# A hybrid decoder layer on one core: both value heads in one product, a shorter inverse root, smaller tiles and a new order

## The chip, the cores and the metric

The kernel runs on one core of a Trainium2 chip. The metric is device time in microseconds (us) of one launch; less is better. Engines are named as in the profile: PE is TensorE's matrix products, PEld its weight loads, DVE is VectorE, ACT is ScalarE, POOL is GpSimd, SP is the queue that issues all DMAs here. PSUM is the memory that products land in, in banks of 128 x 512 float32.

## What is computed

The reference, cut to what the change touches:

```python
h = _rmsnorm(x, norm_w)                    # x: (1, 4096, 1024)
u = (h @ w_in)                             # one projection for both groups
# GLA group: 4 heads, key 64, value 128, chunked, gated
o = _gla_chunked(q, k, v, log_a)
o = o * rsqrt(mean(o*o) + eps) * gla_norm_w
gla_out = o * silu(gg)
# RWKV group: 8 heads of 64, delta rule, step by step over t
kk = kk / max(norm(kk), 1e-12)
S = S*w_t + (S @ -kk_t) (kk_t*a_t)^T + v_t k_t^T ;  y_t = S r_t
y = (y - mean) * rsqrt(var + eps) * ln_w + ln_b
rwkv_out = (y + bonus) * silu(rg)
out = _rmsnorm(x + concat(gla_out, rwkv_out) @ w_out, final_norm_w)
```

The kernel computes the RWKV recurrence in chunks of 64 steps. In a chunk the step-by-step rule becomes products with the inverse of a 64 x 64 triangular matrix, which is called N below.

## The kernel before

**Tiles and stages.** The 4096 positions are cut into 8 blocks of 512 (`TB`). For each block `x_block` normalises x and splits it into a high and a low float16 part; every projection is three float16 products (high by high, high by low, low by high), each of 8 row tiles, for 128 output columns of the weight. A pair of heads is a unit: `rwkv_ab` prepares the 32 RWKV units (8 blocks, 4 pairs), `rwkv_i` finishes the inverse N, `rwkv_c` runs the recurrence over the 8 chunks of a unit, and `rwkv_d` norms its output. `gla_proj` makes keys, queries, values and gates of the 16 GLA units (8 blocks, 2 pairs), and `gla_pair` does their chunks. `out_block` is the output projection, `out_last` that of the last block. The weights are read once, scaled and split by `split_w` and `split_o` in the first part of the program, written to DRAM (`wdr`) and loaded again for each block.

**How products use the array.** `duo` and `both` issue two products that use one half of the array's output columns each (the profile writes 128\*64) and run side by side. The values are made the other way round than all else: x is the stationary operand, and the value weight of one head is the moving one, 128 columns at a time (`gla_proj`, the loop over m, t and the three parts). The transposes use the full array (128\*128), the sums over partitions a quarter (128\*32), the products of 64 rows half of it the other way (64\*128), and the inverse 32\*32.

**The recurrence.** For each chunk `rwkv_c` does three products that hang on each other: `ch<-sv,DD` (state by keys), `ch<-us,Nb` (by N) and `ch<-uv,bk` (new state). Between them ACT copies `us` and `uv` out of PSUM, and DVE makes the next `sv`. N lies in `Nb`, of 192 columns for a chunk: the two heads' blocks stand on the diagonal of a 128 x 128 square with zeros beside them, and the last 64 columns hold a second matrix.

**The inverse.** POOL runs the triangular solve of 32 x 32 blocks (`Tc`, `tm`); its input goes through DRAM (`nd`) and its output through DRAM (`td`, four DMAs) back into `Nb`. `rwkv_i` transposes blocks on DVE (`Ta`) and does two sets of small products.

**The norms.** `newton` makes an inverse square root on DVE from an integer first guess and two Newton steps, eight instructions in all, of 128 x 128. Its result lies in a few rows; `bcast` spreads these over all partitions by DRAM, and `spread` by products with the columns of the tile `sel`, which four small DMAs fill at the start.

**What sets the order.** The code runs as nine streams; a recorder notes each instruction, and a planner gives them the order in which they are issued. Each engine then takes its own in that order and waits on semaphores. The starting times come from a table (`STARTS`), and the planner improves on them with costs of its own. `NW` and `NXR` are numbers of buffers: three of value, key, query and gate weights (`wg`), two of x (`xr`). All recorded instructions stand on line 626 in the profile, or on line 685 when `duo` issues them, so the rows are read by tile.

The values before, with the lines of the profile:

```python
1374            for m in range(2):
1375                i = W_V + 2 * j + m
1376                w = yield from get_w(i)
...
1379                for t in range(4):
1380                    for m_, (a, c) in enumerate(((0, 0), (0, 1), (1, 0))):
...
1383                        for k in range(KT):
...
1385                            both(ps[:, t, :], xs[k][:, c, P * t:P * t + P], w[a][:, k, :], ...
```

Of the kernel before, what the change touches and what calls it, by code (L numbers as in the profile page):

```python
# [1823 lines left out]
```

## Time and profile before

| | |
|---|---|
| median of 3 runs | 2205.69 us (2202.84 to 2206.76) |
| profiled execution, span | 2206.1 us |
| PE busy | 2119.0 us, 96% |
| PEld busy | 1352.7 us, 61% |
| DVE busy | 1711.7 us, 78% |
| ACT busy | 1253.8 us, 57% |
| POOL busy | 875.1 us, 40% |
| DMA | 326.90 MB, 148 GB/s |

The profiled execution has no time of its own beside its span; the span lies 0.4 us above the median of the timed runs and inside their spread, so span and time are read as one here. The share of busy time is an average over parts with different limits, and a matmul's recorded length includes the time in which it drains while the next one already runs.

### The profile page before, as it was taken

What the parts mean: (1) busy time and instruction counts of PE and PEld (TensorE: products, weight loads), DVE (VectorE), ACT (ScalarE), POOL (GpSimd) and SP (SyncE); (2) the same over time, 40 slices, a digit from 0 to 9 for tenths busy, and PEclk for the clock granted to TensorE, in tenths of its full rate; (3) what the DMA queues carried; (4) which work ended last, traced back from release to release, by engine and by line L of the source; (5) the groups of instructions that cost most, each with busy time, mean ns of one, the idle gap of its engine ahead of it and who ended that gap; (6) DMA issues with size and microseconds to landing.
All of it is one profiled execution on the core that took longest, in us unless ns stands there. A gap on an engine that the chain in (4) does not pass through costs nothing.

```text
span 2206.1 us, 75003 instructions
## 1 busy us (share of the span) xinstructions
PE 2119.0 (96%) x30680; PEld 1352.7 (61%) x30680; DVE 1711.7 (78%) x3802; ACT 1253.8 (57%) x3229; POOL 875.1 (40%) x2212
## 2 busy tenths in 40 slices
PE   7888999999999999999999999999999999999997
PEld 3555665566755657556575666656666566756664
DVE  7888969688784977867877886867878578785876
ACT  7766675564645546554654546545465465555452
POOL 3454233625244352335525354441543525254400
PEclk9999999999999999999999999999999999999999
DMA  6786556455344643456444654355544465345443
GB/s 201 230 249 205 182 160 178 141 177 167 91 123 142 184 141 98 115 145 188 138 114 116 183 154 129 101 131 165 164 117 124 127 190 160 90 117 140 130 123 97
DMA packets 275454, 326.90 MB, mean 148 GB/s; under 512 B 131572, under 2 KB 132772, under 8 KB 275108
## 3 DMA queue, kind: packets, MB, share of 16 engines
q1 hardware_dynamic: 275108, 322.10, 50.8%
q8 instruction: 240, 3.93, 0.8%
q14 instruction: 106, 0.87, 0.1%
HBM read 276.94 MB, written 45.05 MB: 146 GB/s over the span
## 4 chain that ended last, share of the span: by engine, by line
PE 66%; DVE 16%; DMA 9%; issue 2%; ACT 2%; SPq 2%; POOL 2%; DVEq 0%; POOLq 0%; ACTq 0%
PE bank L685 52%; PE bank L626 8%; PE ch L685 4%; DMA xr<-in_xT_dram 2%; SPq L626 2%; DVE DD L626 2%; DVE nta L626 1%; DVE bk L626 1%; PE y L626 1%; DMA rn<-bcda 1%; DMA x<-in_wt_dram 1%; PE y L685 1%; DVE mgg L626 1%; DVE x L626 1%; DVE Nb L626 1%
## 5 line engine op out<-in xcount | busy, mean ns | idle before, releaser
L685 PE MATMUL bank<-x,wr 128*64 128x512 f16 x6528 | 796.2, 380 | 7.2 <-ACT x L626 1.4
L626 POOL TENSOR_TENSOR tm<-Tc,f 128x60 f32<-128x60 f32 (+24 forms) x961 | 347.7, 362 | 589.0 <-DMA f<-nd 507.2
L685 PEld LDWEIGHTS <-wr 128*64 128x64 f16 x6528 | 356.1, 110 | 260.1 <-issue 22.1
L626 POOL TENSOR_TENSOR Tc<-Tc,tm 128x60 f32<-128x60 f32 (+24 forms) x961 | 358.2, 373 | 74.1
L685 PE MATMUL bank<-x,wg 128*64 128x512 f16 x3072 | 367.1, 381 | 3.0 <-DMA wg<-wdr 1.9
L685 PE MATMUL bank<-x,wo 128*64 128x512 f16 x2976 | 357.2, 380 | 0.0
L626 POOL TENSOR_TENSOR xacc<-xacc,xr 128x512 f32<-128x512 f32 x98 | 130.8, 1334 | 359.5 <-ACT xr L626 227.9
L685 PEld LDWEIGHTS <-wg 128*64 128x64 f16 x3072 | 169.4, 110 | 126.3 <-issue 5.0
L626 DVE SCALAR_TENSOR_TENSOR sv<-ch,PC,psd 64x64 f32<-64x64 f32 x434 | 122.5, 282 | 160.1 <-PE ch L685 140.6
L685 PEld LDWEIGHTS <-wo 128*64 128x64 f16 x2976 | 159.2, 110 | 112.4 <-issue 2.9
L685 PEld LDWEIGHTS <-x 128*64 128x64 f16 x6240 | 190.1, 111 | 20.8 <-issue 9.0
L685 PE MATMUL bank<-wg,x 128*64 128x128 f16 x6144 | 195.4, 220 | 4.6 <-DMA wg<-wdr 3.0
L626 ACT ACTIVATE psd<-sv,PC 128x128 f32<-128x128 f32 x248 | 98.9, 399 | 139.4 <-DVE sv L626 108.3
L626 ACT COPY uv<-ch 64x64 f32<-64x64 f32 x496 | 102.3, 206 | 76.5 <-PE ch L685 69.5
L626 ACT COPY us<-ch 64x64 f32<-64x64 f32 x496 | 102.2, 206 | 67.8 <-PE ch L685 57.7
L626 ACT ACTIVATE sa<-bank,mu_s 128x512 f32<-128x512 f32 x104 | 71.6, 689 | 73.5 <-PE bank L685 71.1
L626 DVE COPY_PREDICATED Nb<-mc,bank 64x512 f32<-64x512 uint8 x128 | 92.8, 728 | 13.1 <-PE bank L626 11.3
L626 POOL MEMSET Tc<- 32x8 f32 (+1 forms) x160 | 24.2, 151 | 186.1 <-DMA td<-Tc 180.7
L626 DVE COPY_PREDICATED DD<-mc,bank 64x512 f32<-64x512 uint8 x128 | 93.3, 731 | 2.3
L685 PEld LDWEIGHTS ch<-uv,bk 128*64 128x64 f32 x992 | 66.1, 137 | 44.1 <-ACT uv L626 10.9
L685 PEld LDWEIGHTS ch<-us,Nb 128*64 128x64 f32 x992 | 65.4, 137 | 43.0 <-ACT us L626 11.0
L685 PEld LDWEIGHTS ch<-sv,DD 128*64 128x64 f32 x992 | 65.0, 136 | 40.0 <-DVE sv L626 7.3
(348 smaller groups left out, 3611.8 us busy)
## 6 DMA issues: line engine op xcount, KB each, us to landing
wr<-wdr SPq DMA_DIRECT2D x256, 256.0 KB
wg<-wdr SPq DMA_DIRECT2D x184, 256.0 KB
xr<-in_xT_dram SPq DMA_DIRECT2D x176, 256.0 KB
wo<-wdr SPq DMA_DIRECT2D x128, 256.0 KB
f<-nd SPq DMA_DIRECT2D x128, 128.0 KB
x<-in_wt_dram SPq DMA_DIRECT2D x29, 512.0 KB
wdr<-wo SPq DMA_DIRECT2D x25, 512.0 KB
out_dram<-mgg SPq DMA_DIRECT2D x33, 256.0 KB
```

The costliest lines, as they stand in the source:

```text
L626: put(t0, self.name, d, lag, cols, tiles, tab, outs, ins, lambda: f(*a, **kw))
L685: nc.tensor.matmul(x, lhsT=l, rhs=y, start=start, stop=stop)
```

## The change

It makes these edits:

- **Values.** The weights of both heads of a pair are loaded into neighbouring buffers, and one product streams both, 256 columns at a time, for two of the four row tiles in one PSUM bank. The stationary x is loaded once for both heads.
- **Buffers.** Four of `wg` (a value pair takes all four) and three of `xr`.
- **Inverse root.** One integer guess and a polynomial: seven instructions in place of eight.
- **Spread.** The tile `sel`, its memset and its four DMAs are gone; columns of the identity matrix stand in.
- **N.** `Nb` has 128 columns for a chunk. The zeros move into `us`, which holds each head's half beside a zero half; the products keep their number and shape. One DVE transpose of 128 partitions stands where two of 32 were, and one DMA fills `td` where four did.
- **Engines.** Two element-wise steps of each RWKV unit (of `E` and `kf`) go from DVE to ACT. The scale `iv` of the output projection is made once for a block, not once for a tile.
- **Start.** The parameters (`pkt`) may be loaded behind the fourth tile of x.
- **Order.** The planner's search is gone. A table (`ORDER`) ranks every instruction, and they are issued by rank as their inputs allow.

The diff, cut to its core:

```diff
-NW = {"r": 4, "g": 3, "o": 2}
+NW = {"r": 4, "g": 4, "o": 2}
-NXR = 2
+NXR = 3
+ORDER = (
...
+RSQRT = (-568328192.0, 22.474061965942383, -4.702532768249512, 8.77026081085205, -9.808283805847168)
...
-            D.dma_start(sel[q, g, :], ck[q, CK_SEL:CK_SEL + P:64])
...
-        Nb = [sb(un, [P, NC, 192], F32, f"Nb{i}") for i in range(NBUF)]
+        Nb = [sb(un, [P, NC, P], F32, f"Nb{i}") for i in range(NBUF)]
+        us1 = sb(rt, [P, 2, 64], F32, "us")
+        G.memset(us1, 0.0)
...
-            V.tensor_scalar(y.bitcast(I32), v.bitcast(I32), -0.5, float(0x5F1FFFF9), ALU.mult, ALU.add)
-            for a, c in ((-0.703952253, 1.681913948), (-0.5, 1.5000003)):
-                V.tensor_tensor(t, y, y, ALU.mult)
-                V.scalar_tensor_tensor(t, t, a, v, ALU.mult, ALU.mult)
-                V.scalar_tensor_tensor(y, t, c, y, ALU.add, ALU.mult)
+            V.tensor_scalar(y.bitcast(I32), v.bitcast(I32), -0.5, k, ALU.mult, ALU.add)
+            V.tensor_tensor(t, y, y, ALU.mult)
+            V.scalar_tensor_tensor(t, t, z, v, ALU.mult, ALU.mult)
+            V.scalar_tensor_tensor(v, t, a, t, ALU.add, ALU.mult)
+            V.scalar_tensor_tensor(v, v, b, t, ALU.add, ALU.mult)
+            V.scalar_tensor_tensor(y, v, c, y, ALU.add, ALU.mult)
...
-                duo(o, [o[h] for h in (lo, hi)], [sel[:, g, h % heads:h % heads + 1].broadcast_to((P, 64)) for h in range(2)], [rows] * 2, True, True)
+                duo(o, [o[h] for h in (lo, hi)], [ident[:, 32 * g + 16 * h:32 * g + 16 * h + 1].broadcast_to((P, 64)) for h in (0, heads - 1)], [rows] * 2, True, True)
...
-            V.tensor_scalar(E, E, 0.5, 0.5, ALU.mult, ALU.add)
+            S.activation(E, E, AF.Copy, scale=0.5, bias=0.5)
...
-            V.tensor_scalar(kf, ta, hka[:, p:p + 1], hka[:, 4 + p:5 + p], ALU.mult, ALU.add)
+            S.activation(kf, ta, AF.Identity, scale=hka[:, p:p + 1], bias=hka[:, 4 + p:5 + p])
...
-            for g in range(4):
-                D.dma_start(td[:, g].rearrange("m q i -> q m i"), Tc[32 * g:32 * g + 32])
+            D.dma_start(td.rearrange("m g q i -> (g q) m i"), Tc)
...
-            for q0 in (0, 64):
-                V.transpose(Ta[q0:q0 + 32], nb[q0:q0 + 32, :, q0:q0 + 32])
+            V.transpose(Ta, nb[:, :, 0:32])
...
-                both(pc[:, 2, :], nb[:, c, 0:P], us, True, True)
+                duo(pc[:, 2, :], [pc[q_, 2, :] for q_, _, e in two], [nb[:, c, 0:64]] * 2, [us[:, e, :] for _, _, e in two], True, True)
...
+            for t0 in range(0, 4, 2):
+                ps = (yield from need("g")).rearrange("p (t m d) -> p t m d", t=2, m=2)
+                for m_, (a, c) in enumerate(((0, 0), (0, 1), (1, 0))):
+                    for t in range(2):
...
+                            both(ps[:, t], xs[k][:, c, P * (t0 + t):P * (t0 + t) + P], side[a][:, :, k, :], m_ + t + k == 0, m_ == 2 and t == 1 and k == KT - 1)
+                for m in range(2):
+                    i = W_V + 2 * j + m
+                    S.activation(vt[:, t0:t0 + 2, P * m:P * m + P], ps[:, :, m, :], AF.Copy, scale=invs[:, i:i + 1])
...
+            iv = sb(rt, [P, KT], F32, "iv", 2)
+            V.tensor_scalar_mul(iv, woinv, am[:, 1:2])
...
-        for s in sorted(steps, key=lambda s: (start[s.n], s.n)):
+        steps, forward, backward = build(first_guide())
+        rank = order()
```

The first place is PE's queue at the start, from the last products that spread a maximum (`amW`, of the first weights) ahead of the norm's to the first projection (`wr` and `x`). `nyg` is the inverse root of the first block's norm. Before:

```order
L685 LDWEIGHTS amW_211
L685 MATMUL bank_0_189<-identb_109,amW_211 64x128
L685 LDWEIGHTS amW_210
L685 MATMUL bank_0_188<-identb_109,amW_210 64x128
L685 MATMUL bank_0_187<-nyg_208,sel_108 64x128 x8
L685 LDWEIGHTS amW_210
L685 MATMUL bank_0_189<-identb_109,amW_210 64x128
L685 LDWEIGHTS wr_212
L685 MATMUL bank_0_190<-x_0_0_0_83,wr_212 64x512
```

Now:

```order
L901 LDWEIGHTS amW_211
L901 MATMUL bank_0_186<-identb_108,amW_211 64x128
L901 MATMUL bank_0_188<-nyg_209,ident_76 64x128 x8
L901 LDWEIGHTS amW_212
L901 MATMUL bank_0_190<-identb_108,amW_212 64x128
L901 LDWEIGHTS amW_211
L901 MATMUL bank_0_189<-identb_108,amW_211 64x128
L901 LDWEIGHTS wr_213
L901 MATMUL bank_0_191<-x_0_0_0_83,wr_213 64x512
```

Each load and product of a maximum stands twice in the queue, once for each half, and is shown once; so are the loads and products below. The spread of `nyg` stood behind four maxima of weights and ahead of one; now it stands behind two and ahead of two, and it reads the identity, not `sel`.

The second place is PE's queue where the first unit's values begin; `x` is the stationary operand. Before:

```order
L685 LDWEIGHTS x_0_0_0_83
L685 MATMUL bank_0_185<-wg_241,x_0_0_0_83 64x128
L685 LDWEIGHTS x_0_1_0_84
L685 MATMUL bank_0_185<-wg_241,x_0_1_0_84 64x128
L685 LDWEIGHTS x_0_2_0_85
```

Now:

```order
L901 LDWEIGHTS x_0_0_0_83
L901 MATMUL bank_0_187<-wg_185,x_0_0_0_83 64x256
L901 LDWEIGHTS x_0_1_0_84
L901 MATMUL bank_0_187<-wg_185,x_0_1_0_84 64x256
L901 LDWEIGHTS x_0_2_0_85
```

Each load of x is followed by a product of 256 columns, where it was 128. Over the program 3072 such products stand where 6144 stood, and 3168 loads of x where 6240 stood. All other products are the same in number and shape. The changes from one shape of the array to another along PE's queue are 645, and were 661.

The third place is ACT's queue in an RWKV unit of the second block, around the steps of `E` and `kf`; `us`, `uv` and `psd` belong to the recurrence of another unit. Before:

```order
L626 ACTIVATE E_197<-bank_0_189,half_p_118,usc_114 128x512
L626 ACTIVATE sa_220<-bank_0_190,mu_s_121 128x512
L626 COPY us_268<-ch_267 64x64 x2
L626 ACTIVATE ta_198<-bank_0_188,half_p_118,lrs_225 128x512
L626 ACTIVATE xr_221<-mgg_0_92 128x512
L626 ACTIVATE rn_196<-rk_195,pkt_102 128x512
```

Now:

```order
L840 ACTIVATE psd_269<-sv_254,PC_234 128x128
L840 COPY uv_135<-ch_268 64x64 x2
L840 ACTIVATE E_198<-bank_0_186,half_p_117,usc_113 128x512
L840 ACTIVATE E_198<-E_198 128x512
L840 ACTIVATE crs_218<-y_270 128x512
L840 ACTIVATE wo_141<-xr_223,wosc_182 128x512
L840 ACTIVATE ta_199<-bank_0_189,half_p_117,lrs_227 128x512
L840 ACTIVATE kf_200<-ta_199,hka_118 128x512
```

The two added steps stand right behind the ACT instruction that makes their input.

## Rows read from the trace of the kernel before

**Rows 1.** Busy time of each engine in three stretches of the span (start and end in us, length, then busy us and instructions of each engine, granted clock, DMA share, GB/s): the start, the long middle, the end.

```profile
0.00:220.00 220.00, 181.22 (x2342) 109.31 (x2344) 190.49 (x528) 153.89 (x304) 94.42 (x202) 0.96 0.73 221
220.00:2095.00 1875.00, 1844.45 (x26949) 1183.63 (x26945) 1443.37 (x3050) 1053.11 (x2792) 779.97 (x2006) 1.00 0.50 142
2095.00:2206.20 111.20, 93.36 (x1400) 59.81 (x1394) 77.89 (x225) 46.80 (x135) 0.74 (x5) 0.96 0.37 110
```

**Rows 2.** Whom PE waited for in 0 to 220 us: total us, times, the longest.

```profile
PE bank L626 <- DVE bk L626: 6.8, 4, 4.0
PE bank L685 <- ACT wo L626: 5.6, 6, 2.8
...
PE bank L685 <- DVE pw L626: 2.2, 2, 1.8
PE bank L685 <- DMA sel<-in_ck_dram: 1.7, 1, 1.7
```

**Rows 3.** The same in 220 to 2095 us.

```profile
PE ch L685 <- ACT us L626: 4.1, 6, 1.8
PE ch L685 <- ACT uv L626: 3.8, 4, 1.3
PE bank L685 <- DMA wg<-wdr: 3.6, 4, 1.9
PE bank L626 <- POOL xacc L626: 3.3, 3, 1.2
PE bank L626 <- DVE bk L626: 2.1, 3, 1.1
```

**Rows 4.** The timeline of PE where the values of a unit run (start us, length us, engine, line, op, names, shapes, how many are merged in the row).

```profile
298.35 4.66 PE L685 MATMUL bank<-wg,x 128*64 128x128 f16 x160 [0.44 <-DMA wg<-wdr]
302.81 0.31 PE L685 MATMUL ch<-uv,bk 128*64 128x64 f32 x4
```

**Rows 5.** The timeline of PE in a stretch in which the shape of the array changes.

```profile
881.41 0.39 PE L685 MATMUL bank<-lr,uh 128*64 128x512 f16 x2
...
882.06 0.39 PE L685 MATMUL bank<-lr,ul 128*64 128x512 f16 x2
882.38 0.66 PE L626 MATMUL bank<-ident,v 128*128 128x128 f32 x4
```

**Rows 6.** Groups of PE and of its weight loads by shape over the whole span (count, busy us, mean ns of one, idle us before them).

```profile
L685 PE MATMUL bank<-wg,x 128*64 128x128 f16 x6144 | 195.4, 220 | 4.6 <-DMA wg<-wdr 3.0 <-issue 1.5
L685 PEld LDWEIGHTS <-x 128*64 128x64 f16 x6240 | 190.1, 111 | 20.8 <-issue 9.0 <-DMA nd<-Nb 0.2
```

**Rows 7.** A piece of the chain that ended last: the load of a value weight, from its issue to its landing (start us, us).

```profile
294.31 4.00 DMA wg<-wdr
```

**Rows 8.** The timeline of the start.

```profile
11.35 0.29 DVE L626 TENSOR_SCALAR nva<-bank 128x128 f32<-128x128 f32 x1 [6.98 <-PE bank L626]
...
13.65 0.29 DVE L626 SCALAR_TENSOR_TENSOR nyg<-nta,nyg 128x128 f32<-128x128 f32 x1
...
16.52 0.22 DVE L626 TENSOR_SCALAR nwx<-pkt,nwx 128x8 f32<-128x8 f32 x1
...
16.70 0.64 PE L685 MATMUL bank<-nyg,sel 128*64 128x128 f32 x4
...
19.07 1.55 PE L685 MATMUL bank<-nyg,sel 128*64 128x128 f32 x12 [1.73 <-DMA sel<-in_ck_dram]
...
20.67 3.38 DVE L626 SCALAR_TENSOR_TENSOR mgg<-mgg,nwx,bank 128x512 f32<-128x512 f32 x5 [1.83 <-PE bank L685]
...
22.12 0.64 PE L685 MATMUL bank<-x,wr 128*64 128x512 f16 x2 [1.39 <-ACT x L626]
```

**Rows 9.** Groups of DVE by shape over the whole span that the change removes, shortens or moves.

```profile
L626 DVE STREAM_TRANSPOSE Ta<-Nb 32x256 f32<-32x256 f32 x64 | 27.6, 431 | 12.6 <-DMA Nb<-td 11.5
...
L626 DVE TENSOR_TENSOR nta<-nya 128x128 f32<-128x128 f32 x64 | 22.9, 358 | 1.8
...
L626 DVE TENSOR_TENSOR nta<-nyg 128x128 f32<-128x128 f32 x64 | 19.6, 306 | 1.6
...
L626 DVE TENSOR_SCALAR kf<-ta,hka 128x512 f32<-128x512 f32 x32 | 19.2, 599 | 1.6 <-ACT ta L626 1.4
L626 DVE TENSOR_SCALAR E<-E 128x512 f32<-128x512 f32 x32 | 14.4, 449 | 17.6 <-ACT E L626 17.4
...
L626 DVE TENSOR_TENSOR iv<-oam,woinv 128x1 f32<-128x1 f32 x56 | 10.1, 190 | 1.2
```

**Rows 10.** Groups of DVE by shape in 0 to 220 us.

```profile
L626 DVE SCALAR_TENSOR_TENSOR nta<-nta,nva 128x128 f32<-128x128 f32 x14 | 4.2, 300 | 0.3
...
L626 DVE STREAM_TRANSPOSE Ta<-Nb 32x256 f32<-32x256 f32 x4 | 1.7, 432 | 1.5 <-DMA Nb<-td 1.5
...
L626 DVE TENSOR_SCALAR kf<-ta,hka 128x512 f32<-128x512 f32 x3 | 1.6, 522 | 0.0
...
L626 DVE TENSOR_SCALAR E<-E 128x512 f32<-128x512 f32 x3 | 1.2, 416 | 0.0
```

**Rows 11.** Groups of ACT by shape over the whole span.

```profile
L626 ACT COPY us<-ch 64x64 f32<-64x64 f32 x496 | 102.2, 206 | 67.8 <-PE ch L685 57.7 <-DVE x L626 0.3 <-DVE go L626 0.2
...
L626 ACT ACTIVATE sa<-bank,mu_s 128x512 f32<-128x512 f32 x104 | 71.6, 689 | 73.5 <-PE bank L685 71.1 <-DVE pw L626 0.5
...
L626 ACT ACTIVATE vt<-bank,invs 128x512 f32<-128x512 f32 x32 | 21.9, 686 | 27.2 <-PE bank L685 27.0
L626 ACT ACTIVATE E<-E 128x512 f32<-128x512 f32 x32 | 20.1, 627 | 0.7
```

**Rows 12.** The timeline of the end, the last inverse root and its spread.

```profile
2193.72 0.29 DVE L626 TENSOR_SCALAR nva<-ch 128x128 f32<-128x128 f32 x1 [1.21 <-PE ch L626]
...
2196.29 1.09 PE L685 MATMUL bank<-nyg,sel 128*64 128x128 f32 x16 [2.63 <-DVE nyg L626]
```

More of the change, by code (lines that the diff above doesn't have):

```diff
@@ L374, in account, with row @@
             return t0
+        def row(ap):
+            n = 1
+            for step, size in reversed(ap.ap[0 if ap.space == DRAM else 1:]):
+                if step != n and size > 1:
+                    break
+                n *= size
+            return n
         def early(a, b):
@@ L498, in forward @@
                         start[s.n] = t = max(t, flight[-8])
[L499 to L500 removed]
+                    free["H"], free["D"] = t + s.issue, max(t + 0.9, free["D"]) + d
+                    end[s.n] = free["D"] + (late[s.n] if late else 0.0)
                     flight.append(end[s.n] + s.lag)
@@ L536, in backward @@
                 elif e == "D":
-                    hold, long = max(0.5, s.d), s.d + 1.15
+                    hold, long = max(s.issue, s.d), s.d + 0.9
                 free[e], late[s.n] = t + hold, t + long
@@ L626, in call @@
                     put(t0, self.name, d, lag, cols, tiles, tab, outs, ins, lambda: f(*a, **kw))
+                    if self.name == "D":
+                        steps[-1].issue = 0.6 if z == 512 or len(o.shape) > 3 or len(ins[0].shape) > 3 else 0.53 if o.shape[0] == 64 else 0.47 if z == 128 or ins[0].space != DRAM else 0.4
                 return call
@@ L863, in split_w @@
                     yield lambda: got[st] >= k + (st == "g")
-                w = first[i] = pair(st)
+                w = first[i] = pair(st, i)
             split(raw, scl[:, i:i + 1], *w)
@@ L1741, in build @@
         run()
+        for s in reversed(steps):
+            if s.next:
+                for m, lat in s.next.on.items():
+                    if m.n < s.n:
+                        s.follow(m, lat)
+        for s in steps:
+            for m in s.on:
+                m.to.append(s)
         return steps, forward, backward
     with tc.manual_schedule(engines={getattr(mybir.EngineType, e) for e in ("PE", "DVE", "Activation", "Pool", "SP")}):
-        guide, best = first_guide(), None
-        for looks in ROUNDS:
-            steps, forward, backward = build(guide)
-            first_order = forward([s.t0 for s in steps])
-            mine = first_order
-            for keep, look in looks:
-                start, end = first_order
-                for _ in range(PASSES):
-                    start, end = forward(backward(end), keep, look)
-                    mine = min(mine, (start, end), key=lambda x: max(x[1]))
-            if best is None or max(mine[1]) < max(best[2]):
-                best = (steps,) + mine
-            guide = {s.key: (mine[0][s.n], mine[1][s.n]) for s in steps}
-        steps, start, end = best
-        for s in sorted(steps, key=lambda s: (start[s.n], s.n)):
+        steps, forward, backward = build(first_guide())
+        rank = order()
+        left, can = [len(s.on) for s in steps], [(rank[s.n], s.n) for s in steps if not s.on]
+        heapq.heapify(can)
+        while can:
+            s = steps[heapq.heappop(can)[1]]
             s.f()
+            for m in s.to:
+                left[m.n] -= 1
+                if not left[m.n]:
+                    heapq.heappush(can, (rank[m.n], m.n))
 def _layout(d):
```

582 lines of the change are left out of this document (395 added, 187 removed).

## The prediction, made before the changed kernel ran

> **What bounds the kernel now.** I read the busy time of the engines by stretches first, since the page's shares are means over parts with different limits. In the long middle, 220 to 2095 us, PE is busy for 1844.45 of 1875 us, 98.4%; DVE is at 77% and ACT at 56% [rows 1]. So an edit there pays only where it shortens PE's own queue or a wait of PE. At the start, 0 to 220 us, PE is busy for 181.2 us and DVE for 190.5 of 220 (87%), so two engines are close to their limits; at the end PE is idle for 17.8 of 111.2 us. PE's idle time is thus 38.8 + 30.5 + 17.8 = 87 us, and this is all that buffers, faster helpers and a new order could give back, apart from short stalls that the busy time may hide.
>
> The waits came next. At the start PE waits most for `bk` of DVE, 6.8 us, and for ACT's `wo`, 5.6 us [rows 2]. In the middle no wait stands out: `us` 4.1, `uv` 3.8, `wg` 3.6, POOL's `xacc` 3.3 us [rows 3]. Idle time there is spread thin, and an edit that removes one wait finds another close behind it.
>
> **The change part by part.** Times are made against the profiled span, 2206.1 us, which is 0.4 us above the median of the timed runs; I read the two as one.
>
> *Values.* 160 products of 128 columns, in 80 pairs that run side by side, take from 298.35 until the next product at 302.81: 4.46 us, or 55.8 ns a pair [rows 4]. Six products of 512 columns, three pairs, start from 881.41 on and the third pair at 882.06: 0.65 / 3 = 217 ns a pair [rows 5]. No product of 256 columns with this shape of array is in these rows; interpolated it is 55.8 + (217 - 55.8) / 3 = 109.5 ns. Two pairs of 128 become one of 256, which saves 2 x 55.8 - 109.5 = 2.1 ns, 3072 / 2 = 1536 times: 3.2 us, taken as **-3**. The group's whole busy time gives the bound on the good side: 195.4 us [rows 6] against 1536 x 109.5 = 168.2 is -27, if all that the group has above the clean pitch is a cost per load or per product. It also holds waits and the slower clock of the start, so I stay at the run of [rows 4]. On the other side a moving operand in two pieces (two buffers) could cost its few ns back: 0.
>
> What the row shows about loads: each product there has its own load of x, and the pitch is still 55.8 ns. The Trainium skill, "TensorE: Matmul & The Clock Gate", section "Back-to-back issue gap", gives N/2.4 + 2.5 ns for an isolated gap, but for a sustained stream of load and product about 81 ns at 128 columns and 131 at 512. Between these figures 256 columns would take an estimated 98 ns, and halving the loads would save some 64 ns x 1536, near 100 us. The stream of [rows 4] is a sustained one and agrees with the isolated figure; the other is kept as a rival.
>
> *Changes of shape.* After the third pair above, its 217 ns would end at 882.28; the product of the next shape starts at 882.38 [rows 5]: 0.10 us a change. 661 become 645: **-1.6**.
>
> *Start.* Twelve of the sixteen products that spread the first `nyg` waited 1.73 us for `sel`, until 19.07 us, though `nyg` was done at 13.94; the first `mgg` came at 20.67 and the first projection at 22.12 [rows 8]. With the identity nothing waits for a small DMA. The sixteen take 0.64 + 1.55 = 2.2 us, so from about 14.0 they end near 16.2; what is late next is `nwx`, done at 16.74, which `mgg` also needs. So `mgg` starts near 17.0, not 20.67. **-3.5** (0 if the first weights' maxima, now more of them behind the spread, or their splits are late next; at best -4.5).
>
> *Setup, 0 to 220 us.* DVE loses `kf` 1.6, `E` 1.2, half of `Ta` 0.8 and 7 inverse roots of one step less, 7 x 0.30 = 2.1 [rows 10]: 5.7 us. PE waits there for DVE's `bk` and `pw`, 9.0 us [rows 2], so most of it can reach PE: **-4** (0 to -5.7).
>
> *Middle.* DVE loses over the whole span, from [rows 9]: `E` 14.4, `kf` 19.2, half of `Ta` 13.8, one step of 306 to 358 ns in each of 96 inverse roots (three such groups of 64, two to a root; the third isn't shown) 32, and most of `iv`, 48 of 56, 9.1: 88 us, of which some 82 lie behind the setup; 77% becomes 73%. ACT gains `E` 20.1, `kf` 32 x 0.69 = 22 (as `sa`, same shape with one operand for each partition), and `vt` in 64 pieces of 256 columns: between 206 ns at 64 and 686 at 512 that is 0.41 us, 26.4 for 21.9. Sum +47 us [rows 11]: 56% becomes 58.5%. Neither bounds, so I count none of it by itself. What it can do is shorten PE's idle 30.5 us. For the order and the buffers I counted in the two queues how many loads of `wg` have under 4.5 us of PE's products (at the pitches above) between the last use of the old tile and the first of the new, where a load takes 4.00 us [rows 7]: 11 of 189 before, 5 of 188 now. The 3.6 us of waits for `wg` should about halve. Much of the rest, `us`, `uv`, `bk`, `xacc`, is distance between steps of the recurrence and of the setup, which the new order can better or worsen. I take a third of the idle time: **-9**, between -30 (all of it) and +21 (below).
>
> Here stands a rule against the change. `E` takes 449 ns on DVE and 627 on ACT; `kf` takes 599 there, and a like step 689 on ACT [rows 9, 11]. The Trainium skill, "ScalarE: Activation LUTs", section "Rules for kernel authors", says that additions and multiplications belong on VectorE. In engine time the rows agree, 42 us of ACT for 34 of DVE; in the middle ACT has more room, so by the rows the move costs the span nothing, while by the rule it should not have been made.
>
> *End.* The last `nyg` comes out of eight steps from 2193.72 until its spread starts at 2196.29, with PE idle 2.63 us [rows 12]: 0.32 a step. One step less there and in the norm ahead of it: **-0.7**.
>
> *At nothing.* `td` in one DMA and the third `xr` buffer only lighten SP and DMA, which are half idle (share 0.50, [rows 1]); at worst a `td` that lands later delays `Nb`, whose use stands several products of other units away. The products of `N` keep number and shape; zeros moved into `us` leave its copies at 64 columns. The fourth `wg` buffer buys less than it says, since a value pair takes all four and a gate's weights can be loaded only when the values are through; the count of short reloads above holds that.
>
> Sum: -3 - 1.6 - 3.5 - 4 - 9 - 0.7 = -21.8, so **2184 us**.
>
> **Rivals.**
> *Middle and setup give nothing.* For it: in the middle each wait is below 0.25% of the span and is in a queue behind others. Then -8.8 is left, 2197 us, and with the start held up by its weights' DMAs 2201: faster by little, or the same.
>
> *Loads pace the values.* If the load of x and not the column count sets the time of many values' products, the bound of -27 comes in place of -3: 2206.1 - 27 - 18.8 = 2160. The long-run figure of the skill's "Back-to-back issue gap" leads here. For it: the group's busy time is 63.6 ns a pair, 7.8 above the clean run (195.4 / 3072); against it: [rows 4]. The same time comes out if two thirds or more of the middle's idle time and more than the listed setup goes.
>
> *Slower: ACT stands in front of the recurrence.* The 64 added steps of 0.63 to 0.69 us stand right behind the steps that make their input, in the same queue as the copies `us` and `uv` for which PE waits between two products of a chunk. Where a copy becomes ready just behind such a step, PE waits up to 0.66 us. If half of the 64 added steps each hold up PE for that long, it is 32 x 0.66 = +21 us in place of -9: 2206.1 - 12.8 + 21 = 2214. From about 20 of 64 it eats all that the other terms give. For it: `us` and `uv` already lead the waits of the middle. Against it: they held PE up only 10 times, 7.9 us [rows 3], with 496 copies of `us` alone [rows 11], though ACT was at 56% with steps of that length.
>
> **How the numbers follow.** The forecast, 2184 with its own range of 2168 to 2196, gets 0.52. Deeper, near 2160, 0.16, of which the loads that pace the values have 0.06. Middle and setup without a gain 0.24: 0.15 at some 2197, and 0.09 inside the 0.2% (4.4 us) that a measurement of this kernel can tell from no change. Slower 0.08. Faster 0.52 + 0.16 + 0.15 = **0.83**, same **0.09**, slower **0.08**. The range leaves out the lower half of the deep case, and the slower one with part of the same: **2160 to 2204**.
>
> **What would show it.** Right: the values' run at about 109 ns a pair; the first projection near 18.5 us, not 22.1; PE's idle time in the three stretches near 31, 21 and 17 us; ACT near 1300 and DVE near 1625 us busy; no waits for `us` and `uv` above some 8 us. Wrong: a pitch of the values far below 109 ns, or a PE group well under 168 us, makes the loads the cause; `us` and `uv` above 20 us with an `E` or `kf` ahead of them make it ACT; `wg` waits that grow make it the value pair that takes all four buffers; an idle middle that stays at 30 us means that the order gave nothing. What would make the whole forecast wrong is the middle's idle time, which I sized by a share and not by a row.

## The result, and the profile of the changed kernel

| | before | changed |
|---|---|---|
| median | 2206.23 us (4 runs) | 2175.19 us (4 runs, 2169.20 to 2179.29) |
| ratio, 95% interval | | 0.9861 [0.9842, 0.9881] |
| span of the profiled execution | 2206.1 us | 2167.4 us |
| PE busy | 2119.0 us | 2102.0 us |
| DVE busy | 1711.7 us | 1633.6 us |
| ACT busy | 1253.8 us | 1297.9 us |

The change takes 31 us off the median, 1.4%; 2184 was forecast, with a range of 2160 to 2204. The profiled execution is the fastest of the four, 2169.20 us, and its span lies 1.8 us below that. By the same 1.8 us the profiled execution before, of 2206.1 us by its span, took near 2208, and not the 2206.1 that the forecast read as a time. So the spans differ by 38.7 us where the medians differ by 31: the parts that are read below from one execution of each kernel add up to 8 us too much.

The busy time by stretches, as in [rows 1]; the middle and the end are shifted so that the last 111 us form the end again.

```profile
0.00:220.00 220.00, 184.61 (x2132) 111.39 (x2134) 194.34 (x528) 160.95 (x316) 92.38 (x202) 0.91 0.74 232
220.00:2056.40 1836.40, 1823.29 (x24211) 1173.40 (x24209) 1364.04 (x2824) 1089.45 (x2873) 788.29 (x2011) 1.00 0.50 144
2056.40:2167.40 111.00, 94.11 (x1274) 58.13 (x1269) 75.23 (x212) 47.49 (x136) 0.00 (x0) 0.96 0.34 101
```

PE's idle time is 35.4, 13.1 and 16.9 us, where it was 38.8, 30.5 and 17.8. Of the 38.7 us, 21.7 are idle time, 17.4 of them in the middle; the other 17.0 come out of PE's busy time. The granted clock at the start is lower than before, 0.91 for 0.96: of the first 220 us, 37.5 run at 1.2 GHz in place of 2.4, and 17.1 did before. PE is busy for 27.86 and 12.54 us of these; the sums over them, now and before:

```profile
sum 37.50, PE 27.86 PEld 12.57 DVE 33.44 ACT 29.35 POOL 15.81; mean PE 5.57 PEld 2.51 DVE 6.69 ACT 5.87 POOL 3.16
```

```profile
sum 17.10, PE 12.54 PEld 10.44 DVE 16.40 ACT 11.65 POOL 6.63; mean PE 6.27 PEld 5.22 DVE 8.20 ACT 5.83 POOL 3.32
```

In the middle the execution before had two more such stretches of 3.4 us, with PE busy throughout; the changed one has none.

```profile
1310.00:1313.42 3.42, 3.42 (x24) 2.03 (x22) 3.33 (x6) 1.48 (x5) 1.44 (x3) 0.50 0.23 61
1903.92:1907.34 3.42, 3.42 (x71) 3.19 (x67) 3.34 (x6) 1.71 (x3) 0.00 (x0) 0.50 0.54 195
```

If work takes twice as long at half the clock, the lower clock held PE up for an estimated 14 us now (half of 27.9) and 10 before (half of 12.5 + 6.8).

Whom PE waited for from 220 to 2060 us, as in [rows 3]:

```profile
PE bank L901 <- DVE DD L840: 4.2, 6, 2.3
PE ch L901 <- DVE sv L840: 1.0, 2, 0.5
PE bank L840 <- DVE Ta L840: 0.9, 2, 0.6
PE bank L901 <- ACT Nb L840: 0.8, 1, 0.8
```

The rows that led before, `us` 4.1, `uv` 3.8, `wg` 3.6 and `xacc` 3.3, are gone from the list. `DD` has grown to their size, 4.2 us, where it was:

```profile
PE bank L626 <- DVE DD L626: 1.9, 2, 1.6
```

The values and their loads, as in [rows 6], and one group whose products didn't change; first that group as it was before:

```profile
L626 PE MATMUL bank<-DD,bk 64*128 64x128 f32 x1024 | 76.0, 290 | 10.2 <-DVE bk L626 8.9 <-ACT go L626 0.8 <-DVE SC L626 0.2
```

```profile
L901 PE MATMUL bank<-wg,x 128*64 128x256 f16 x3072 | 192.0, 273 | 2.3 <-DVE DD L840 2.3
L901 PEld LDWEIGHTS <-x 128*64 128x64 f16 x3168 | 169.5, 110 | 17.3 <-issue 7.3
...
L840 PE MATMUL bank<-DD,bk 64*128 64x128 f32 x1024 | 67.9, 279 | 0.7 <-DVE bk L840 0.7
```

The values' group fell by 3.4 us. A group's busy time also holds what runs between its products. Counted from each product's start to the next product's, without recorded idle time, the values take 169.9 us for 177.3. Of the 177.3, an estimated 1.4 us are the lower clock, for 50 of the products.

1024 products of `DD` and `bk`, the same in number and shape, are booked with 8.1 us less, and their idle time with 9.5 less. Most of the 8.1 is the clock too. 69 of these products ran at 1.2 GHz before, in whole or in part, and none does now. 32 of them took 189.95 - 185.39 = 4.56 us, 143 ns each (`x` by `wg` follows at 189.95), with a granted clock of 0.50:

```profile
180.20:190.40 10.20, 8.14 (x80) 6.63 (x82) 9.96 (x18) 8.61 (x23) 0.73 (x5) 0.50 0.57 172
185.39 4.64 PE L626 MATMUL bank<-DD,bk 64*128 64x128 f32 x32 [1.55 <-DVE bk L626]
```

Now 32 such products are booked with 2.06 us in one run of the middle:

```profile
264.16 2.06 PE L840 MATMUL bank<-DD,bk 64*128 64x128 f32 x32
```

Outside the slow stretches the time from one start to the next, without idle time, is 66.3 ns before and 64.3 now. So 69 x (145 - 66) ns, some 5.4 us, is the clock.

The run of a unit's values, as in [rows 4]:

```profile
275.65 5.30 PE L901 MATMUL bank<-wg,x 128*64 128x256 f16 x94
280.78 0.39 PE L901 MATMUL bank<-x,wr 128*64 128x512 f16 x2
```

47 pairs take 280.78 - 275.65 = 5.13 us, 109.1 ns a pair; 109.5 was interpolated.

The start, as in [rows 8]:

```profile
10.18 0.63 ACT L840 ACTIVATE rn<-mgg 128x512 f32<-128x512 f32 x1 [1.52 <-DMA mgg<-in_xT_dram]
...
11.51 0.63 ACT L840 ACTIVATE ta<-mgg 128x512 f32<-128x512 f32 x1 [0.70 <-DMA mgg<-in_xT_dram]
...
14.62 0.29 DVE L840 TENSOR_SCALAR nva<-bank 128x128 f32<-128x128 f32 x1 [0.27 <-PE bank L840]
...
16.80 0.28 DVE L840 SCALAR_TENSOR_TENSOR nyg<-nva,nyg 128x128 f32<-128x128 f32 x1
...
17.14 1.09 PE L901 MATMUL bank<-nyg,ident 128*64 128x128 f32 x16
...
20.79 2.48 PE L901 MATMUL bank<-x,wr 128*64 128x512 f16 x8 [0.72 <-ACT wr L840]
```

The spread follows `nyg` at once, where it stood 2.8 us behind the maxima and then waited 1.73 us for `sel`. From `nva` to the first projection it takes 6.17 us, where it took 10.77: 4.6 us less. But two of the eight squares of x wait for their tile until 10.18 and 11.51 us, and `nva` starts at 14.62, not 11.35. The first projection comes 1.33 us earlier.

PE sums the eight squares in the same order as before: `rk`, `rn`, `E`, `ta`, `kf`, `r`, `v`, `uv`. ACT now makes `rn` and `ta` last, so on PE the sums of squares long done stand behind theirs. First now, then the last square and its sum before:

```profile
10.86 0.65 PE L840 MATMUL bank<-rn,gtwo 128*32 128x128 f32 x8 [4.30 <-ACT rn L840]
...
12.20 0.65 PE L840 MATMUL bank<-ta,gtwo 128*32 128x128 f32 x8 [0.25 <-ACT ta L840]
...
13.90 0.65 PE L840 MATMUL bank<-uv,gtwo 128*32 128x128 f32 x8
```

```profile
9.95 0.63 ACT L626 ACTIVATE uv<-mgr 128x512 f32<-128x512 f32 x1 [0.17 <-DMA mgr<-in_xT_dram]
10.63 0.65 PE L626 MATMUL bank<-uv,gtwo 128*32 128x128 f32 x8
```

From the last square's start to `nva` it takes 14.62 - 11.51 = 3.1 us now and 11.35 - 9.95 = 1.4 before; so 1.7 of the 3.3 us is this order. The other 1.6 is the last square's later start. The eight loads of x are issued by 4.5 us in both kernels; when the last one lands differs from one execution to the next (under the same table its square starts at 9.55 us in newt_six below).

The end, as in [rows 12]:

```profile
2155.04 0.29 DVE L840 TENSOR_SCALAR nva<-ch 128x128 f32<-128x128 f32 x1 [1.21 <-PE ch L840]
...
2157.28 1.09 PE L901 MATMUL bank<-nyg,ident 128*64 128x128 f32 x16 [2.31 <-DVE nyg L840]
```

From `nva` to the spread it is 2.24 us for 2.57, one step of 0.33 less.

The groups of ACT that the change made or moved, as in [rows 11]:

```profile
L840 ACT ACTIVATE vt<-bank,invs 128x256 f32<-128x256 f32 x64 | 28.0, 471 | 26.6 <-PE bank L901 26.1
...
L840 ACT ACTIVATE kf<-ta,hka 128x512 f32<-128x512 f32 x32 | 25.9, 810 | 0.5
```

Both are longer than I took them to be, 471 ns for 412 and 810 for 689.

### The profile page after: what moved, and what is told of

It is laid out like the page before. It is cut to its first block, busy times and chain, and to the rows that moved or that the text cites. A ratio compares the mean times of both kernels' runs of the same rounds, so it can differ in the third digit from the quotient of the medians.

```text
span 2167.4 us, 68604 instructions
## 1 busy us (share of the span) xinstructions
PE 2102.0 (97%) x27608; PEld 1342.9 (62%) x27608; DVE 1633.6 (75%) x3563; ACT 1297.9 (60%) x3325; POOL 880.7 (41%) x2212
## 4 chain that ended last, share of the span: by engine, by line
PE 83%; DVE 9%; DMA 3%; ACT 2%; issue 1%; SPq 0%; POOL 0%; DVEq 0%; ACTq 0%
PE bank L901 66%; PE bank L840 10%; PE ch L901 4%; PE y L840 1%; DVE DD L840 1%; PE y L901 1%; DVE bk L840 1%; DVE mgr L840 1%; DVE mgg L840 1%; DVE Nb L840 1%; DMA wdr<-wo 1%; DMA xr<-in_xT_dram 0%; DVE nva L840 0%; DVE crs L840 0%; DVE x L840 0%
## 5 line engine op out<-in xcount | busy, mean ns | idle before, releaser
L901 PEld LDWEIGHTS <-wr 128*64 128x64 f16 x6528 | 361.7, 110 | 265.4 <-issue 27.1
L840 POOL TENSOR_TENSOR Tc<-Tc,tm 128x60 f32<-128x60 f32 (+24 forms) x961 | 371.1, 386 | 73.1
L901 PE MATMUL bank<-x,wg 128*64 128x512 f16 x3072 | 377.3, 381 | 2.0 <-ACT wg L840 0.8
L840 DVE SCALAR_TENSOR_TENSOR sv<-ch,PC,psd 64x64 f32<-64x64 f32 x434 | 122.5, 282 | 188.7 <-PE ch L901 151.8
L901 PEld LDWEIGHTS <-wo 128*64 128x64 f16 x2976 | 163.8, 110 | 115.5 <-issue 4.8
L901 PE MATMUL bank<-wg,x 128*64 128x256 f16 x3072 | 192.0, 273 | 2.3 <-DVE DD L840 2.3
L901 PEld LDWEIGHTS <-x 128*64 128x64 f16 x3168 | 169.5, 110 | 17.3 <-issue 7.3
L901 PEld LDWEIGHTS ch<-us,Nb 128*64 128x64 f32 x992 | 66.7, 137 | 35.4 <-ACT us L840 3.9
```

What stands on the lines that cost most here:

```text
L840: put(t0, self.name, d, lag, cols, tiles, tab, outs, ins, lambda: f(*a, **kw))
L901: nc.tensor.matmul(x, lhsT=l, rhs=y, start=start, stop=stop)
```

## The experiments

My theory was that the middle's gain is the work of the new order and the buffers, since neither DVE nor ACT bounds anything there. The rival: the lighter DVE is the gain. A second rival: the loads of x paced the values. Where a difference between two kernels is told in the text, it is the difference of their ratios to the kernel before, times 2206 us; with intervals of about 0.2% on each, some 6 us between two of them can't be told from nothing.

| kernel | median, us | ratio, 95% interval | PE idle in the middle, us |
|---|---|---|---|
| changed | 2175.19 | 0.9861 [0.9842, 0.9881] | 13.1 |
| split_values | 2181.05 | 0.9893 [0.9873, 0.9912] | 17.7 |
| ekf_dve | 2199.20 | 0.9969 [0.9955, 0.9982] | 34.0 |
| ekf_late | 2186.00 | 0.9913 [0.9894, 0.9931] | 18.4 |
| newt_iv | 2200.22 | 0.9971 [0.9958, 0.9984] | 32.2 |
| newt_six | 2169.74 | 0.9839 [0.9826, 0.9851] | 14.1 |
| act_twice | 2189.28 | 0.9928 [0.9916, 0.9940] | 25.4 |
| planner | 2187.82 | 0.9920 [0.9898, 0.9942] | 24.3 |
| old_order | 2184.82 | 0.9901 [0.9881, 0.9920] | 22.8 |
| planner_xr2 | 2185.62 | 0.9915 [0.9902, 0.9928] | 22.5 |
| before_ekf_act | 2206.51 | 1.0003 [0.9989, 1.0017] | 32.8 |
| xr_two | 2345.42 | 1.0636 [1.0613, 1.0658] | 129.3 |
| order_rest | 2408.83 | 1.0909 [1.0884, 1.0934] | 170.1 |

The last column leaves out the first 220 and the last 111 us of each profiled execution; the kernel before has 30.5 there. It is from one execution of each kernel, and these lie up to 6 us off their kernel's median, so small differences in it say nothing.

**split_values.** The wide product is cut in two again; nothing else moves on any queue.

```diff
-both(ps[:, t], x, side[a][:, :, k, :], ...)
+for m in range(2):
+    both(ps[:, t, m], x, side[a][:, m, k, :], ...)
```

> The changed kernel with each value product of 256 columns cut into two of 128, one for each head, so that x is loaded once for each head again; everything else, the order of all engines too, as in the changed kernel. By the columns (my prediction's term): 55.8 ns a pair twice against 109.5, 2.1 ns x 1536 = 3 us more than the changed kernel's 2175, about 2178. If the loads of x paced the values before, 20 to 30 us more, 2195 to 2205.

Its ratio is 0.3% above the changed kernel's (7 us), with intervals that overlap. The group of values, from the groups by shape:

```profile
L788 PE MATMUL bank<-wg,x 128*64 128x128 f16 x6144 | 198.9, 220 | 3.9 <-DVE DD L727 2.3 <-issue 1.3
```

198.9 for 192.0 us, 6.9 more. It is nearer to the 3 us of the columns than to the 20 to 30 of the loads, which fall away as a rival. Counted from start to start, as above, the values take 176.6 us here for 169.9, of which an estimated 1.4 us are the lower clock again (55 products): 5 to 6 us, a little more than the columns give.

**ekf_dve.** `E` and `kf` on DVE, each at the place in the order behind ACT's tanh.

```diff
-S.activation(E, E, AF.Copy, scale=0.5, bias=0.5)
+V.tensor_scalar(E, E, 0.5, 0.5, ALU.mult, ALU.add)
...
-S.activation(kf, ta, AF.Identity, scale=hka[:, p:p + 1], bias=hka[:, 4 + p:5 + p])
+V.tensor_scalar(kf, ta, hka[:, p:p + 1], hka[:, 4 + p:5 + p], ALU.mult, ALU.add)
```

> The changed kernel with the two steps of E and kf back on DVE, each right behind the step that makes its input; the orders of all other instructions as in the changed kernel. If the middle's gain is from the order and the buffers, DVE has room for 34 us in 2000 and the time is 0 to 5 us above the changed kernel's 2175, most of that in the setup. If the lighter DVE is what took PE's waits away, 15 us or more above. If ACT is what holds up the recurrence now, a few us below.

24 us above the changed kernel, against my 0 to 5. The groups by shape and a piece of DVE's timeline:

```profile
L724 DVE TENSOR_SCALAR kf<-ta,hka 128x512 f32<-128x512 f32 x32 | 18.8, 588 | 23.0 <-ACT ta L724 23.0
...
L724 DVE TENSOR_SCALAR E<-E 128x512 f32<-128x512 f32 x32 | 15.9, 496 | 38.1 <-ACT E L724 38.1
```

```profile
1015.54 1.00 DVE L724 TENSOR_SCALAR E<-E 128x512 f32<-128x512 f32 x1 [4.11 <-ACT E L724]
1016.46 0.57 DVE L724 SCALAR_TENSOR_TENSOR sv<-ch,PC,psd 64x64 f32<-64x64 f32 x2
```

DVE stands still until ACT's tanh is through, once for 4.11 us, and the recurrence's `sv` stands behind it in the same queue. PE's waits for `sv` from 220 to 2060 us grow from 1.0 to 13.7 us. This says that the place was bad for a step on DVE, not yet what DVE's own time costs.

**ekf_late.** The same two steps, each directly ahead of the DVE step that reads its result.

> The changed kernel with the two steps of E and kf on DVE, each directly ahead of the DVE step that reads its result (the scan of E, the product of kf), where DVE waited for ACT's result anyhow; all other orders as in the changed kernel. In ekf_dve DVE stood idle 38.1 us ahead of E and 23.0 ahead of kf, waiting for ACT's tanh. If this waiting in DVE's queue was what cost 24 us there, it is mostly gone now: 2176 to 2184. If DVE's own 35 us are what counts, it stays near 2195 to 2200.

11 us above the changed kernel, just over the 2176 to 2184 of the hand-over and far from the 2195 of DVE's own time. DVE now stands 3.8 and 1.0 us ahead of `E` and `kf`, where it stood 38.1 and 23.0. About half of ekf_dve's 24 us, 12 with an uncertainty of some 6, was the waiting in the queue.

**newt_iv.** Eight steps for an inverse root, and `iv` for each tile. DVE has plain work more, no hand-over.

```diff
+V.tensor_tensor(t, y, y, ALU.mult)
...
-V.tensor_scalar_mul(iv, woinv, am[:, 1:2])
+V.tensor_tensor(iv, am[:, 1:2], woinv[:, n:n + 1], ALU.mult)
```

> The changed kernel with the inverse root of eight steps (a second Newton step) and the scale iv made for each tile, so that DVE has some 40 us more of plain work, with no hand-over between engines more; the orders of PE, ACT and SP as in the changed kernel. If DVE has room and only hand-overs count: the setup's 2 us and 0.7 at the end, 2177 to 2181. If a lighter DVE is the gain of the middle, in proportion to its 88 us of relief 10 to 15 us: 2185 to 2190.

24 us, more than either case gave. Whom PE waited for, over the whole span, in this kernel and then in the changed one:

```profile
PE ch L785 <- DVE sv L724: 13.0, 18, 1.8
```

```profile
PE ch L901 <- DVE sv L840: 4.5, 7, 1.1
```

DVE is 75.1% busy in the middle, and 74.3% in the changed kernel; the share hardly moves. What moves is `sv`, which now comes late for PE 18 times, and 7 times in the changed kernel. This is 8.5 us of the 24; the rest isn't traced.

**newt_six.** One step less than the changed kernel in each root: a quadratic, `v = (s + a) s`, `y = (v + c) y`.

```diff
-V.scalar_tensor_tensor(v, v, b, t, ALU.add, ALU.mult)
```

> The changed kernel with one step less again in each of the 96 inverse roots: a quadratic in place of the cubic, six instructions, good to 2.6e-5; DVE has 31 us less, the orders of all engines are otherwise as in the changed kernel. In newt_iv 41 us more on DVE cost 25. If a lighter DVE is worth that much at any level, 10 to 20 us less: 2155 to 2165. If the table of ranks fits DVE's present lengths and only more work hurts, 2170 to 2176.

5 us below the changed kernel, with intervals that overlap, and PE's idle time in the middle no smaller (14.1 for 13.1). So 25 us less on DVE (1608.5 busy for 1633.6) give little, where 36 us more (1669.4, newt_iv) cost 24. So the time does not follow DVE's busy time in proportion. This alone doesn't refute the rival: a lighter DVE could give much up to a point and little beyond it.

**before_ekf_act.** The kernel before with this one edit; its own search plans again.

```diff
-V.tensor_scalar(E, E, 0.5, 0.5, ALU.mult, ALU.add)
+S.activation(E, E, AF.Copy, scale=0.5, bias=0.5)
...
-V.tensor_scalar(kf, ta, hka[:, p:p + 1], hka[:, 4 + p:5 + p], ALU.mult, ALU.add)
+S.activation(kf, ta, AF.Identity, scale=hka[:, p:p + 1], bias=hka[:, 4 + p:5 + p])
```

> The kernel before with one edit: the two steps of E and kf on ACT; its own search plans the order anew. If DVE's relief and the hand-over that goes with it (17.4 us of DVE waiting for ACT ahead of E in the kernel before) are worth their time without the new order too, 8 to 15 us less than 2206: 2191 to 2198. If they only count under the new order, 2203 to 2208. If ACT in front of the recurrence costs, over 2208.

No difference: 1.0003 [0.9989, 1.0017]. By itself, under the old plan, the move from DVE to ACT gives nothing and costs nothing.

**act_twice.** The two steps on ACT, each followed by a copy onto itself.

```diff
 S.activation(E, E, AF.Copy, scale=0.5, bias=0.5)
+S.activation(E, E, AF.Copy, scale=1.0, bias=0.0)
...
+S.activation(kf, kf, AF.Copy, scale=1.0)
```

> The changed kernel with each of the two steps that went to ACT followed by a copy of its result onto itself (scale 1), so that ACT has 64 steps or some 40 us more and DVE, PE and the orders are as they were. My slower rival put the price of such steps, standing in front of us and uv, at up to 0.33 us each: 21 us, near 2196. If ACT at 60% has room, 2175 to 2180. The chain through E and kf is also 0.63 us longer a step.

15 us for 64 steps. Over the whole span PE waits for these copies:

```profile
PE ch L785 <- ACT us L724: 4.5, 8, 1.0
PE ch L785 <- ACT uv L724: 3.6, 8, 0.8
```

In the changed kernel it is 0.6 and 1.6 over the whole span. So my slower rival's mechanism is real, and it is 6 us by these waits. The middle's idle time grew by 12.3 us; what the rest is isn't traced, and longer steps under a table that was made without them are a rival here as in newt_iv.

**planner.** All edits, but the search of the kernel before in place of the table of ranks.

```diff
-rank = order()
...
+start, end = forward(backward(end), keep, look)
...
+for s in sorted(steps, key=lambda s: (start[s.n], s.n)):
+    s.f()
```

> All edits of the change, but the issue order made by the search of the kernel before (the same two looks of five passes) from the new table of starting times, in place of the table of ranks. If the table of ranks is the gain, 2190 to 2205; if the edits and the new starting times are, 2175 to 2185.

It falls between the two cases, 13 us above the changed kernel: that much is the table's.

**old_order.** As planner, and the starting times are those of the kernel before, step by step.

> All edits of the change, with the starting times of the kernel before (step by step, those of both heads' values spread over the time that the two heads' products had) and its search. What the order is worth beside the edits: by my theory some 20 us of the middle are lost, 2190 to 2200. If the edits alone make the gain, 2175 to 2182. If the value pair, which takes all four weight buffers, needs an order made for it, PE waits for wg after each unit's queries, up to 16 x 4 us, and the time is over 2215.

2184.8 us. The edits under the old plan give 22 us of the 31, and PE's idle time in the middle falls from 30.5 to 22.8. The new order is worth the other 9, with an uncertainty of some 6. So most of the gain is the edits', the buffers among them, and my theory had put too much on the order. The value pair that takes all four buffers needs no order made for it: PE's waits for `wg` in the middle are 3.5 us (2 times), and were 3.6.

**xr_two.** Two buffers of `xr` under the table of ranks.

```diff
-NXR = 3
+NXR = 2
```

> The changed kernel with two buffers of xr in place of three, under the same table of ranks. I counted the third buffer at nothing: within 2 us of 2175. If it is what took away PE's waits for POOL's sum of squares (xacc, 3.3 us in the middle before), 3 to 6 us above.

2345 us, 170 more. Whom DVE waited for (the first of these is 151.8 us in the changed kernel too, the second is not in its list):

```profile
DVE sv L723 <- PE ch L784: 187.9, 127, 5.8
DVE xr L723 <- DMA xr<-in_xT_dram: 56.6, 20, 7.4
```

DVE now stands 56.6 us at steps whose `xr` has not landed, and ACT 64.2 us ahead of its squares of `xr` (13.6 in the changed kernel), with all that the table ranks behind them. The two spans differ by 177 us, all of it in the middle: 116 are idle time of PE, and 61 are PE's busy time, 1883.95 us for 1823.29, at a granted clock of 0.97 for 1.00. PE was busy at 1.2 GHz for 94 us of it, and half of that, an estimated 47 us, is the clock:

```profile
220.00:2233.30 2013.30, 1883.95 (x24298) 1206.67 (x24299) 1377.89 (x2860) 1096.76 (x2895) 784.31 (x2016) 0.97 0.46 132
```

**planner_xr2.** Two buffers as well, but the search plans for them.

> All edits of the change but the third buffer of xr, with the order made by the search from the new starting times, as in planner (2187.8), so that the order can fit two buffers. If the third buffer is worth nothing by itself, 2186 to 2190; if the 170 us of xr_two are the buffer and not the table that was made for three, far over 2200.

2185.6 us, not to be told from planner's 2187.8. The third buffer is worth nothing by itself; the 170 us are the table's, which was made for three.

**order_rest.** The table of ranks with the wide product, both moves, the short root, `iv` and the third `xr` undone together.

> The changed kernel's table of ranks, its layout of N, its four weight buffers and its identity columns, with the rest undone: value products of 128 columns for each head, E and kf on DVE, the inverse root of eight steps, the scale iv made for each tile, two buffers of xr. By my theory the new order is most of the gain and the undone parts are worth 3 (values), 4 to 6 (setup) and 1 (end), with little in the middle: 2182 to 2188. If the lighter engines are the gain and the order is not, 2195 or more.

2409 us. It was meant to weigh the order alone, but the lost third buffer governs it, as in xr_two; it decides nothing between order and edits.

## Why the prediction held, point by point

- **PE bounds, and only its work or its waits count.** Right: 98.4% of the middle before, 99.3% now.
- **Values, -3.** The pitch was right, 109.1 ns for 109.5. The term was too small: counted from start to start the values fell by some 6 us at equal clock, and cutting them again costs 5 to 6 so counted (7 in the time, with an uncertainty of about 6). That loads pace the values is refuted. The sustained figures of the Trainium skill ("TensorE: Matmul & The Clock Gate", "Back-to-back issue gap"), by which the values would have given near 100 us, don't hold here; the isolated gap does.
- **Changes of shape, -1.6.** Not measured by itself.
- **Start, -3.5.** Mis-sized as a whole: 1.3. The part of it that I worked out gave 4.6, since nothing waits for `sel` and the spread stands behind fewer maxima. What I left out is the way to `nva`, which starts 3.3 us later: 1.7 because the new order squares the second and the fourth tile of x last, and 1.6 because the last tile is squared later, which is in part chance. My sum held no term for the order of the loads and squares. Under the old plan (old_order) the first projection comes at 18.01 us, near the 18.5 that I gave.
- **Setup, -4.** Start and setup together were to take 7.5 us off PE's idle time in the first 220; it is 3.4, and 6.5 under the old plan (old_order). The clock is a term that I had left out: PE was busy at 1.2 GHz for 27.9 us of this stretch where it was for 12.5, an estimated 8 us lost on top. How much of this is the change is open; newt_six, under the same table, has a clock of 0.95 there.
- **Middle, -9.** The step that was mis-sized most, as I had said it might be: 17.4 us of idle time went, not 9. A third of the idle time was a share that I picked and not a row, so that the total came within 9 us is luck in part: the start and the setup gave less than forecast and the middle more. PE's busy time fell by 17.0 over the span where values and shapes were to give 4.6; the values took some 6 of this and the clock's shift in the group of `DD` and `bk` some 5, while the clock as a whole cost more than before. The rest is spread over other products and isn't traced. That busy time hides short stalls, as I had allowed, is not shown. Under the old plan (old_order) 7.7 of the 17.4 go, under the new one the rest, by one execution of each.
- **"Neither bounds, so I count none of it by itself."** This is shown for `E` and `kf` in the kernel before with its plan made anew: 2206.5. It fails under a fixed table, where 24 us come back for 36 of plain DVE work. The rule of the Trainium skill ("ScalarE: Activation LUTs", "Rules for kernel authors") that additions belong on VectorE would have had the move cost; in the span it didn't.
- **ACT's added time.** `kf` takes 810 ns on ACT, not the 689 of `sa`: it has two operands for each partition where `sa` has one. The Trainium skill ("ScalarE: Activation LUTs", "What ACT_TABLE_LOAD costs") gives 186 ns + 0.833 ns an element and some 93 ns for each such operand, by which it would be an estimated 799; the trace agrees. In all ACT is 44 us busier, where 47 were forecast.
- **End, -0.7.** 0.33 in the last root, and 0.9 us less idle time in the end's stretch.
- **At nothing, the third `xr` buffer.** True for a plan made for two, 2185.6; under the table it is worth 170 us. I priced the buffer, and the change had built its order on it.
- **Slower, ACT in front of the recurrence.** It did not happen: in the middle, waits for `us` and `uv` are no longer listed. For 64 further steps (act_twice) I had 21 us, and they cost 15, of which 6 are traced to these copies.

What stays open: which edits gave the 7.7 us of the middle under the old plan (the short root, `iv`, the transposes and the fourth `wg` buffer were not tried apart under a new plan), and why roots that are 0.3 us longer, with `iv` made for each tile, cost as much as 24 us under the table. newt_iv shows where some of it lands, at `sv`. Whether the lighter DVE is what made room for the new order, no run tells. That the table was fitted to the lengths of the steps is what the asymmetry with newt_six suggests, and no run proves it.

## What to carry to other kernels

An order that is fixed in a table is a part of every other edit: undo one under the table and you measure the misfit (a buffer that is worth nothing showed as 170 us), so weigh an edit with the order made anew, as in old_order and planner_xr2. An engine at 75% that feeds a chain of dependent steps can cost time by what stands ahead of the chain's step in its queue, long before it is full. And when the order changes, follow the start through every queue: a load that moved to the end holds up all that the next engine has ranked behind it. When a group's busy time changes and its products don't, look at the granted clock under them first.

## What was not expected

A group's busy time can change with the clock alone: 69 of the 1024 products of `DD` and `bk` stood in slow stretches before, at 145 ns from start to start, where the others took 66. At the start the mean granted clock, of stretches at 2.4 and at 1.2 GHz, fell from 0.96 to 0.91; PE is busy for about as long as before (184.6 and 181.2 us of 220), but for 15 us more of it at the lower clock. xr_two shows it at its largest: PE stood idle for 129.3 us of the middle, and was busy at the lower clock for 94 us of it, where the changed kernel had no such stretch there.
